# Accumulating DMAs at the end of the expert mixture, and normed rows stored in k-tile order

## The chip, the core and the metric

The kernel runs on one core of one Trainium2 chip. The metric is device time in microseconds (us) of one execution, median of several runs. Five engines work side by side, each through its own queue in order: TensorE (PE, with its weight loads as PEld), VectorE (DVE), ScalarE (ACT), GpSimd (POOL) and SyncE (SP), which here only issues DMAs. Sixteen DMA engines move data between DRAM and SBUF.

## What is computed

Two stacks one after the other on 512 tokens of width 1024, all in f32. The change touches the first stack, two layers of attention followed by a mixture of experts:

```python
for l in range(DEPTH):                       # DEPTH = 2
    ...                                      # three kinds of attention, concatenated to mix
    x = layer_norm(DEEPNORM_ALPHA * x + einsum('bsm,md->bsd', mix, w_out[l]), ln1_g[l], ln1_b[l])
    x = layer_norm(DEEPNORM_ALPHA * x + moe_ffn(x, w_router, router_bias, w_gate[l], w_up[l], w_down[l]), ln2_g[l], ln2_b[l])

def moe_ffn(x, ...):                         # 16 experts of width 256, two of them for each token
    scores = sigmoid(xt @ w_router)
    ...                                      # best group of four experts, best two in it, gates that sum to 1
    h = silu(einsum('nd,edf->enf', xt, w_gate)) * einsum('nd,edf->enf', xt, w_up)
    y = einsum('enf,efd->nd', h * gates, w_down)
```

The second stack (pooling, dilated attention, four wide feed-forward blocks) follows and is not touched.

## The kernel before, in words

Tokens lie in four tiles `t` of 128 rows (`X[:, t, :]`, 128x1024 f32). Most products are made of three passes (`mm3`, L205): weights are split by ACT and DVE into a high and a low part (`split`, L201 to L203; the tile is called `hl`), and TensorE does high by high, high by low, low by high. Plain f32 products and transposes go through TensorE directly.

A mixture layer (`moe`, L625) runs in four steps.

Route (L694 to L709): as soon as a tile of `X` is normed, SP stores it to DRAM (`x1d`, L699), TensorE transposes its eight 128x128 blocks (L705), ACT copies them to `x1T` (L706), and TensorE multiplies with the router's weights (L708). `x1T` lives in buffers tagged `xg`, four in the first layer and three in the second (`XG`). The choice of experts then runs on DVE with small products, up to `tok_of`, the list of rows for each expert.

Experts (L903 to L914): for each of 16 experts POOL gathers up to 96 rows of `x1d` with an indirect DMA (L823), `turn` (L827) transposes them in eight pieces, `widen` (L839) makes gate and up, `shift` (L871) transposes the 96x256 result in two pieces, `narrow` (L881) multiplies with `w_down`, ACT scales by the gates, and POOL scatters the rows to `yd` in DRAM (L893): the first choices in rows 0 to 511, the second choices in rows 512 to 1023. Weights are loaded so that a partition holds neighbouring rows (`"(p k) m"`, L680), so the piece `k` of a gathered row is every eighth of its elements, and the piece `f` of `h1` every second:

```python
xg = xgs.pop(e).rearrange("p (q k) -> p k q", k=KD)      # L829
PE.transpose(ps[...], xg[:, 4 * h + k, :], ident)        # L834
h1 = h1.rearrange("p (q f) -> p f q", f=2)               # L874
PE.transpose(ps[...], h1[:, f, :], ident)                # L876
```

Combine (L926 to L932): eight PSUM banks `acc[t, h]` are started with alpha times X (L924). For each tile `t` and each choice `j` SP loads 128 rows of `yd` (512 KB) and TensorE adds them to both halves `h` by a product with the identity (L932), 16 plain f32 products of 128x512 in a layer. The second choice's rows go to a buffer of `row_tile(t)` (L861): tags `y`, `y`, and for `t = 2` in the second layer `gain`, then `y` again. `self.hold` keeps the last of these loads; the weight loads of what follows (`wload`, L178) are issued behind it on SP's queue. All of `yd`'s loads wait for the last scatter.

Norm and feed (L934 to L942): `norm(t)` is bn_stats on both halves (L577), then a chain over DVE and POOL (L590, L591), or over DVE, ACT and POOL for tiles 1 and 2 of the first layer (L585 to L587). `feed(t)` (in the second layer after a second norm with `gain`) transposes the tile (L222) and splits it into `xt`, the operand of the next stage. The order is written out in `ENDS` (L42): first layer `c0 c1 n0 c2 n1 f0 c3 n2 f1 n3 f2 f3`, second `c0 c1 n0 n1 f0 f1 c2 c3 n2 n3 f2 f3`; a scheduler places the instructions of each engine within what the dependencies allow.

Of the kernel before, what the change touches and what calls it, by code (L numbers as in the profile page):

```python
# [9 lines left out]
F32 = mybir.dt.float32  # L10
# [4 lines left out]
OP = mybir.AluOpType  # L15
AX = mybir.AxisListType

P = 128
S = 512
T = S // P  # L20
D = 1024
KD = D // P
# [15 lines left out]
XG = 4, 3  # L38
# [12 lines left out]
CAP = 96  # L51
# [58 lines left out]
class Core:  # L110
# [514 lines left out]
    def moe(self, l, mix, mp, then):  # L625
        nc, a, c, tc = self.nc, self.a, self.c, self.tc
        V, A, PE, G = nc.vector, nc.scalar, nc.tensor, nc.gpsimd
# [47 lines left out]
        def fetch(n):  # L675

            for _ in range(n):
                w, e = need.pop(0)
                raw = next(places)
                src = a[w][l, e].rearrange("(p k) m -> p k m", p=P)  # L680
                k = src.shape[1] // 2
                if isinstance(raw, list):
                    ready[w, e] = [self.wload(src[:, h * k:(h + 1) * k], raw[h]) for h in range(2)]
                else:
                    v = self.wload(src, raw)
                    ready[w, e] = [v[:, :k], v[:, k:]]
# [7 lines left out]
        def route(t):  # L694

            X = self.X
            if t == 0:
                fetch(RAW + 5)
            nc.sync.dma_start(self.x1d[t * P:(t + 1) * P, :], X[:, t, :])  # L699
            lg = self.bank()[:NE, :P]  # L700
            x1T = mp.tile([P, KD, P], F32, name="x1T", tag="xg", bufs=XG[l])
            for h in range(2):
                ps = self.bank("t")
                for k in range(4):
                    PE.transpose(ps[:, k * P:(k + 1) * P], X[:, t, (4 * h + k) * P:(4 * h + k + 1) * P], self.ident)  # L705
                (V.tensor_copy if t == T - 1 and h else A.copy)(x1T[:, 4 * h:4 * h + 4, :], ps.rearrange("p (k q) -> p k q", q=P))  # L706
            for k in range(KD):
                PE.matmul(lg, wr[:, k, :], x1T[:, k, :], start=k == 0, stop=k == KD - 1)  # L708
            A.activation(scT[:, t * P:(t + 1) * P], lg, AF.Sigmoid)  # L709
        self.attn_out(l, mix, mp, route)  # L710
        X = self.X
# [40 lines left out]
        for t in range(T + 1):  # L752
            o = rk[:, t * NE:(t + 1) * NE]
# [14 lines left out]
        for j in range(2):  # L768
            for t in range(T):
                PE.matmul(sm_ps[:CAP, :3 * NE], hot[j][:, t, :], vals[:, j, t].rearrange("p a e -> p (a e)"),  # L770
                          start=j + t == 0, stop=j + t == T)
# [46 lines left out]
        xgs, ready_x = {}, {}  # L818
# [7 lines left out]

        def turn(e):  # L827

            xg = xgs.pop(e).rearrange("p (q k) -> p k q", k=KD)  # L829
            xgT = [mp.tile([P, KD, CAP], F32R, name=f"xgT{i}") for i in range(2)]  # L830
            for h in range(2):
                ps = self.bank("t")[:, :4 * CAP]
                for k in range(4):
                    PE.transpose(ps[:, k * CAP:(k + 1) * CAP], xg[:, 4 * h + k, :], self.ident[:CAP, :CAP])  # L834
                v = ps.rearrange("p (k q) -> p k q", q=CAP)
                self.split(xgT[0][:, 4 * h:4 * h + 4], xgT[1][:, 4 * h:4 * h + 4], v)
            ready_x[e] = xgT
# [23 lines left out]
        def row_tile(e):  # L861
            if e % 3 < 2:
                return mp.tile([P, D], F32, name="y", tag="y", bufs=2)
            if l == 0:
                return mp.tile([P, D], F32, name="y", tag="more2")
            return self.norm.tile([P, D], F32, name="y", tag="gain", bufs=2)
# [4 lines left out]
        def shift(e, h1):  # L871

            ps = self.bank("t")[:, :2 * CAP]
            h1 = h1.rearrange("p (q f) -> p f q", f=2)  # L874
            for f in range(2):
                PE.transpose(ps[:, f * CAP:(f + 1) * CAP], h1[:, f, :], self.ident[:CAP, :CAP])  # L876
            hT = [mp.tile([P, 2 * CAP], F32R, name=f"hT{i}", tag=f"hT{i}", bufs=2) for i in range(2)]
            self.split(hT[0], hT[1], ps)
            return e, hT
# [40 lines left out]
        acc = {}  # L920
        for t in range(T):
            for h in range(2):
                acc[t, h] = self.bank("at"[h])
                PE.matmul(acc[t, h], alpha, X[:, t, h * 512:(h + 1) * 512], start=True, stop=False)  # L924

        def combine(t):  # L926
            for j in range(2):
                yg = row_tile(t) if j else mp.tile([P, D], F32, name="yg", tag="xg", bufs=XG[l])
                i = nc.sync.dma_start(yg, self.yd[j * S + t * P:j * S + (t + 1) * P, :])
                self.hold = i.ins  # L930
                for h in range(2):
                    PE.matmul(acc[t, h], self.ident, yg[:, h * 512:(h + 1) * 512], start=False, stop=j == 1)  # L932

        def norm(t):  # L934
            with tc.issue_after(fed[1]) if t >= HOLD[l] else nullcontext():
# [40 lines left out]
    def rest_experts(self, l, mp, rp, slots):  # L976
        nc, a, tc = self.nc, self.a, self.tc
        V, A, PE, G = nc.vector, nc.scalar, nc.tensor, nc.gpsimd
        with tc.For_i(0, NE, 1) as e:
            one = bass.ds(e, 1)  # L980

            def weights(w, m, h):
                t = mp.tile([P, 1024], F32, name="wrest", tag="xg", bufs=XG[l])
                src = a[w][l, one].rearrange("o (k p) m -> p (o k) m", p=P)
                n = 1024 // m
                nc.sync.dma_start(t.rearrange("p (k m) -> p k m", m=m), src[:, h * n:(h + 1) * n, :])
                return t
# [502 lines left out]
```

## Time and profile before

| | |
|---|---|
| time, median of 3 runs | 2852.64 us (2850.58 to 2852.91) |
| the profiled execution | 2854.86 us, its span 2853.0 us |
| PE busy | 2761.9 us, 97% of the span |
| weight loads (PEld) busy | 2287.9 us, 80% |
| DVE, ACT, POOL busy | 1526.5, 1180.2, 233.0 us |
| chain that ended last | PE 63%, DVE 3%, ACT 1%, POOL 1% |
| TensorE's mean granted clock | 0.983 |

The profiled execution is 2.22 us above the median. Its span is the time from the first to the last instruction. A busy PE is not PE at its peak, since matmuls overlap; the pace of a row of equal instructions is read from the start of one to the start of the next.

### The profile page before, as it was taken

The numbers are of one execution on the slowest core, as the hardware profiler recorded it, in microseconds if no ns is written. First come the engines' busy times: TensorE is split into PE (matmuls) and PEld (weight loads), VectorE is DVE, ScalarE is ACT, GpSimd is POOL, SyncE is SP. The second block draws the span as 40 slices with busy tenths as digits, with TensorE's granted clock in tenths as the row PEclk, the third lists the DMA queues.
The fourth block names the chain that finished last, engine by engine and source line by source line (L and its number), as shares of the span: only waits on it lengthen the run. The fifth ranks groups of instructions, "written<-read, shape, count | busy, mean of one in ns | idle before, by whom it ended". The sixth has DMA issues, their size and how long they took to land.

```text
span 2853.0 us, 35973 instructions
## 1 busy us (share of the span) xinstructions
PE 2761.9 (97%) x14092; PEld 2287.9 (80%) x14092; DVE 1526.5 (54%) x2819; ACT 1180.2 (41%) x2133; POOL 233.0 (8%) x233
## 2 busy tenths in 40 slices
PE   8998999998999999999999999999999999999998
PEld 7767986766996888888888887998888787888886
DVE  7975987976896323356533337343233635632334
ACT  4373883373894222234423224232322445532222
POOL 0031211041211000010100001000000000100000
PEclk9999999999999999999999999999999999999999
DMA  4316976215985223323322333333232314133220
GB/s 168 76 45 228 349 274 216 60 39 218 322 334 194 99 90 104 101 68 125 98 94 89 104 103 108 133 122 104 90 102 94 106 42 138 52 104 103 95 93 33
DMA packets 176159, 365.06 MB, mean 128 GB/s; under 512 B 14544, under 2 KB 115152, under 8 KB 164592
## 3 DMA queue, kind: packets, MB, share of 16 engines
q1 hardware_dynamic: 165424, 336.35, 35.1%
q0 software_dynamic: 9984, 25.31, 2.6%
q8 instruction: 112, 1.84, 0.3%
q10 hardware_dynamic: 576, 1.05, 0.1%
q14 instruction: 63, 0.52, 0.1%
HBM read 343.73 MB, written 27.33 MB: 130 GB/s over the span
## 4 chain that ended last, share of the span: by engine, by line
PE 63%; DVE 3%; ACT 1%; issue 1%; POOL 1%; POOLq 0%; DVEq 0%; ACTq 0%
PE psa L207 17%; PE psa L209 17%; PE psa L208 17%; PE pst L207 3%; PE pst L209 3%; PE pst L208 3%; PE psa L1295 1%; PE pst L1323 1%; DVE xn L241 1%; POOL rr L1045 1%; DVE hl L203 1%; PE pst L222 1%; PE pst L1313 0%; DVE X L1060 0%; PE pst L1243 0%
## 5 line engine op out<-in xcount | busy, mean ns | idle before, releaser
L203 DVE TENSOR_TENSOR hl<-raw,hl 128x1024 fp32r<-128x1024 f32 (+2 forms) x451 | 552.6, 1232 | 776.5 <-ACT hl L202 774.3
L202 ACT CAST hl<-raw 128x1024 fp32r<-128x1024 f32 (+1 forms) x456 | 471.7, 1042 | 685.7 <-PE psa L209 331.6
L209 PE MATMUL psa<-xt,hl 128*128 128x512 f32 (+1 forms) x1632 | 603.9, 370 | 1.9 <-DVE hl L203 1.9
L207 PE MATMUL psa<-xt,hl 128*128 128x512 f32 (+1 forms) x1632 | 603.7, 370 | 0.7 <-ACT xt L202 0.7
L208 PE MATMUL psa<-xt,hl 128*128 128x512 f32 (+1 forms) x1632 | 604.1, 370 | 0.2 <-DVE xt L203 0.2
L209 PEld LDWEIGHTS psa<-xt,hl 128*128 128x128 f32 x1632 | 310.3, 190 | 53.8 <-DVE hl L203 2.3
L207 PEld LDWEIGHTS psa<-xt,hl 128*128 128x128 f32 x1632 | 310.1, 190 | 52.3 <-ACT xt L202 1.1
L208 PEld LDWEIGHTS psa<-xt,hl 128*128 128x128 f32 x1632 | 310.3, 190 | 51.8 <-DVE xt L203 0.8
L207 PE MATMUL psa<-hl,xt 128*128 128x512 f32 (+2 forms) x608 | 244.8, 404 | 3.1 <-ACT hl L202 3.1
L209 PE MATMUL psa<-hl,xt 128*128 128x512 f32 (+2 forms) x608 | 245.1, 403 | 0.0
L208 PE MATMUL psa<-hl,xt 128*128 128x512 f32 (+2 forms) x608 | 241.2, 397 | 3.1 <-DVE hl L203 3.0
L1096 ACT ACTIVATE silu<-psa 128x512 f32<-128x512 f32 x88 | 52.6, 597 | 345.8 <-PE psa L209 345.8
L207 PE MATMUL psa<-hl,hT 128*128 128x512 f32 (+1 forms) x480 | 189.0, 394 | 0.0
L208 PE MATMUL psa<-hl,hT 128*128 128x512 f32 (+1 forms) x480 | 187.8, 391 | 0.0
L209 PE MATMUL psa<-hl,hT 128*128 128x512 f32 (+1 forms) x480 | 187.8, 391 | 0.0
L1097 DVE TENSOR_TENSOR silu<-silu,psa 128x512 f32<-128x512 f32 x88 | 60.5, 687 | 218.3 <-PE psa L209 217.9
L1045 POOL TENSOR_TENSOR rr<-ms,consts 128x1 f32<-128x1 f32 x52 | 38.6, 744 | 1637.1 <-DVE ms L1043 1625.9
L207 PEld LDWEIGHTS psa<-hl,xt 128*128 128x128 f32 x608 | 139.2, 229 | 21.1 <-issue 3.3
L208 PEld LDWEIGHTS psa<-hl,xt 128*128 128x128 f32 x608 | 139.5, 229 | 18.6 <-DVE hl L203 5.3
L209 PEld LDWEIGHTS psa<-hl,xt 128*128 128x128 f32 x608 | 139.1, 229 | 13.3 <-issue 1.0
L207 PE MATMUL psa<-hl,xgT 128*96 128x256 f32 x512 | 145.5, 284 | 0.2
L209 PE MATMUL psa<-hl,xgT 128*96 128x256 f32 x512 | 143.3, 281 | 0.0
(365 smaller groups left out, 4420.6 us busy)
## 6 DMA issues: line engine op xcount, KB each, us to landing
raw<-in_ffn_w_gate_dram SPq DMA_DIRECT2D x44, 1024.0 KB
raw<-in_ffn_w_up_dram SPq DMA_DIRECT2D x44, 1024.0 KB
raw<-in_ffn_w_down_dram SPq DMA_DIRECT2D x44, 1024.0 KB
raw<-in_w_up_dram SPq DMA_DIRECT2D x16, 1024.0 KB
raw<-in_w_gate_dram SPq DMA_DIRECT2D x12, 1024.0 KB
raw<-in_w_down_dram SPq DMA_DIRECT2D x12, 1024.0 KB
xt<-in_w_down_dram SPq DMA_DIRECT2D x12, 1024.0 KB
xt<-in_w_gate_dram SPq DMA_DIRECT2D x10, 1024.0 KB
```

The source lines that it names most:

```text
L202: self.nc.scalar.copy(hi, src)
L203: return (self.nc.gpsimd if pool else self.nc.vector).tensor_tensor(lo, src, hi.bitcast(F32), op=OP.subtract)
L207: mm(out, lhs[0], rhs[0], start=start, stop=False)
L208: mm(out, lhs[0], rhs[1], start=False, stop=False)
L209: mm(out, lhs[1], rhs[0], start=False, stop=stop)
L222: self.nc.tensor.transpose(ps[:, k * P:(k + 1) * P], src[:, (4 * h + k) * P:(4 * h + k + 1) * P], self.ident)
L241: self.nc.vector.scalar_tensor_tensor(o, i, r, gh, op0=OP.mult, op1=OP.mult)
L1045: nc.gpsimd.tensor_tensor(r, ms, self.c("nhalf")[:, :1], op=OP.pow)
L1096: A.activation(s, acc[0], AF.Silu)
L1097: V.tensor_tensor(s, s, acc[1], op=OP.mult)
L1295: PE.matmul(ps[:, (j - j0) * nk + b * P:(j - j0) * nk + (b + 1) * P], qT[half(par), j, :], kv["k", g, kb][half(par), j, :], start=True, st ...
L1323: PE.matmul(o[half(par), j * P:(j + 1) * P], v[:, (2 * j + par) * 64:(2 * j + par + 1) * 64], pts[b][:, j * P:(j + 1) * P], start=b == 0, ...
```

## The change

- `route`: ACT copies each normed tile into a new tile `xp` (128x1024, tag `xg`) in which element `q * 8 + k` of a row stands at place `k * 128 + q`, and SP stores `xp` to `x1d` instead of `X`. The store now stands behind the copies to `x1T`.
- `turn` and `shift`: the transposes read pieces of 128 neighbouring elements. To fit, `w_down` is loaded as `"(k p) m"`: two runs of 4 KB for each partition in place of one of 8 KB.
- Combine: the four tiles of first choices are loaded into `sums[t]` (three buffers `xg`, one `y`), one load behind the other on SP; then POOL issues four DMAs that add the second choices' rows to them in SBUF (`accum_op=add`). TensorE adds one tile to each bank: 8 plain f32 products in a layer, not 16. `self.hold` is now the last of the four loads.
- `moe_rest` (only for experts with more than 96 rows) is adapted to the new order of rows.

```diff
-                src = a[w][l, e].rearrange("(p k) m -> p k m", p=P)
+                src = a[w][l, e].rearrange("(k p) m -> p k m" if w == "w_down" else "(p k) m -> p k m", p=P)
...
-            nc.sync.dma_start(self.x1d[t * P:(t + 1) * P, :], X[:, t, :])
...
+            xp = mp.tile([P, KD, P], F32, name="xp", tag="xg", bufs=XG[l])
+            A.copy(xp, X[:, t, :].rearrange("p (q k) -> p k q", k=KD))
+            nc.sync.dma_start(self.x1d[t * P:(t + 1) * P, :], xp.rearrange("p k q -> p (k q)"))
...
-            xg = xgs.pop(e).rearrange("p (q k) -> p k q", k=KD)
+            xg = xgs.pop(e)
...
-                    PE.transpose(ps[:, k * CAP:(k + 1) * CAP], xg[:, 4 * h + k, :], self.ident[:CAP, :CAP])
+                    PE.transpose(ps[:, k * CAP:(k + 1) * CAP], xg[:, (4 * h + k) * P:(4 * h + k + 1) * P], self.ident[:CAP, :CAP])
...
-            h1 = h1.rearrange("p (q f) -> p f q", f=2)
-                PE.transpose(ps[:, f * CAP:(f + 1) * CAP], h1[:, f, :], self.ident[:CAP, :CAP])
+                PE.transpose(ps[:, f * CAP:(f + 1) * CAP], h1[:, f * P:(f + 1) * P], self.ident[:CAP, :CAP])
...
+        sums = [mp.tile([P, D], F32, name="yg", tag="xg", bufs=XG[l]) if t < 3 else row_tile(0) for t in range(T)]
+        for t in range(T):
+            i = nc.sync.dma_start(sums[t], self.yd[t * P:(t + 1) * P, :])
+            self.hold = i.ins
+        for t in range(T):
+            G.dma_start(sums[t], self.yd[S + t * P:S + (t + 1) * P, :], accum_op=OP.add)
+
         def combine(t):
-            for j in range(2):
-                yg = row_tile(t) if j else mp.tile([P, D], F32, name="yg", tag="xg", bufs=XG[l])
-                i = nc.sync.dma_start(yg, self.yd[j * S + t * P:j * S + (t + 1) * P, :])
-                self.hold = i.ins
-                for h in range(2):
-                    PE.matmul(acc[t, h], self.ident, yg[:, h * 512:(h + 1) * 512], start=False, stop=j == 1)
+            yg = sums[t]
+            for h in range(2):
+                PE.matmul(acc[t, h], self.ident, yg[:, h * 512:(h + 1) * 512], start=False, stop=True)
```

## Rows read from the trace of the kernel before

**Rows 1.** Windows: stretch; us, busy time (instructions) of each engine, PEclk, DMA share, GB/s.

```profile
276.00:430.00 154.00, 153.64 (x1130) 139.24 (x1131) 131.60 (x164) 131.81 (x187) 27.74 (x29) 0.98 0.84 304
430.00:456.00 26.00, 23.42 (x61) 10.50 (x60) 11.56 (x21) 5.07 (x8) 5.38 (x6) 0.93 0.83 300
```

**Rows 2.** Groups by line and shape, PEld: count, busy us, mean ns, idle before.

```profile
L834 PEld LDWEIGHTS pst<-consts,xg 96*128 96x128 f32 x256 | 31.9, 203 | 13.0 <-issue 13.0
...
L876 PEld LDWEIGHTS pst<-consts,h 96*128 96x128 f32 x64 | 10.3, 196 | 0.2
...
L705 PEld LDWEIGHTS pst<-consts,X 128*128 128x128 f32 x64 | 7.2, 140 | 1.4 <-issue 0.8
```

**Rows 3.** Timeline of TensorE, bursts of transposes: start us, us, instruction, idle before.

```profile
254.26 1.58 PE L705 MATMUL pst<-consts,X 128*128 128x128 f32 x13
...
263.29 0.26 PEld L714 LDWEIGHTS psa<-consts,scoresT 16*128 16x128 f32 x3 [0.21 <-issue]
...
420.26 0.32 PEld L876 LDWEIGHTS pst<-consts,h 96*128 96x128 f32 x2
420.47 0.19 PEld L207 LDWEIGHTS psa<-hl,xgT 128*96 128x96 f32 x1
...
851.51 0.98 PEld L834 LDWEIGHTS pst<-consts,xg 96*128 96x128 f32 x8
852.38 0.19 PEld L207 LDWEIGHTS psa<-hl,hT 128*96 128x96 f32 x1
```

**Rows 4.** Timelines of ACT and POOL, route stage of the first layer.

```profile
252.46 1.05 ACT L202 CAST hl<-early 128x1024 fp32r<-128x1024 f32 x1 [3.18 <-PE pst L209]
...
258.37 0.58 ACT L706 COPY x1T<-pst 128x512 f32<-128x512 f32 x1 [0.21 <-PE pst L705]
...
260.80 0.58 ACT L706 COPY x1T<-pst 128x512 f32<-128x512 f32 x1 [0.32 <-PE pst L705]
...
271.92 1.25 POOL L823 DMA_INDIRECT xg<-x1d,tok_of  x1 [14.55 <-DVE tok_of L781]
```

**Rows 5.** Timelines of SP, PE and DVE, end of the first layer's mixture.

```profile
434.70 0.33 SPq L929 DMA_DIRECT2D yg<-yd  x1
...
444.16 3.31 SPq L188 DMA_DIRECT2D raw<-in_w_in_dram  x4
...
438.32 1.73 PE L932 MATMUL psa<-yg,consts 128*128 128x512 f32 x2 [2.05 <-DMA yg<-yd]
...
449.56 1.02 PE L932 MATMUL pst<-y,consts 128*128 128x512 f32 x2
450.42 0.60 PE L222 MATMUL pst<-consts,X 128*128 128x128 f32 x4
...
442.89 0.70 DVE L577 BATCH_NORM_STATS2 st<-psa 128x6 f32<-128x512 f32 x1 [15.31 <-PE psa L932]
...
446.29 1.28 DVE L591 SCALAR_TENSOR_TENSOR X<-X,rstd,gb 128x1024 f32<-128x1024 f32 x1
```

**Rows 6.** Timelines of PE, SP and DVE, end of the second layer's mixture.

```profile
875.90 1.12 PE L932 MATMUL psa<-yg,consts 128*128 128x512 f32 x2 [2.00 <-DMA yg<-yd]
...
886.50 0.33 SPq L247 DMA_DIRECT2D gain<-in_norm_gain_dram  x1
...
878.78 0.70 DVE L577 BATCH_NORM_STATS2 st<-psa 128x6 f32<-128x512 f32 x1 [13.57 <-PE psa L932]
...
893.66 0.68 DVE L249 TENSOR_SCALAR gain<-gain 128x1024 f32<-128x1024 f32 x1
894.26 1.22 DVE L203 TENSOR_TENSOR hl<-raw,hl 128x1024 fp32r<-128x1024 f32 x1
```

**Rows 7.** Windows (columns as in the first group), after the first combine load landed.

```profile
438.00:440.00 2.00, 1.68 (x3) 0.78 (x4) 0.00 (x0) 0.00 (x0) 0.00 (x0) 0.68 1.03 420
```

**Rows 8.** Tile `x2d`: POOL's 512 KB stores, ns min/median/max, then time to landing.

```profile
L942 POOL DMA_DIRECT2D x2d<-X x4: 538/594/630, 447.9 to 465.9; - x4
...
DMA to landing us min/median/max: 3.5/5.4/7.3
```

More of the change, by code (lines that the diff above doesn't have):

```diff
@@ L983, in weights @@
                 t = mp.tile([P, 1024], F32, name="wrest", tag="xg", bufs=XG[l])
-                src = a[w][l, one].rearrange("o (k p) m -> p (o k) m", p=P)
+                src = a[w][l, one].rearrange("o (k p) m -> p (o k) m" if w == "w_down" else "o (p k) m -> p (o k) m", p=P)
                 n = 1024 // m
```

## The prediction

> **What bounds the kernel now.** The page says TensorE, 97% busy, and the chain that ended last is mostly PE. That is an average, so the second view is the one by stage. In the experts' stretch PE is busy 153.64 of 154 us, ACT 131.81, DVE 131.60, and the DMA engines have a share of 0.84 [rows 1]; the second layer's stretch, 714 to 868 us, repeats it. There every instruction that leaves TensorE shortens the kernel, until ACT or DVE, 14% below, become the bound. In the 26 us at the end of the first mixture PE is busy 23.42 us and DVE 11.56 [rows 1], but the timeline shows an order in it: PE waits 2.05 us for the first rows of `yd`, DVE waits 15.31 us for the first finished bank, and only then does the chain of norms start which the next stage needs [rows 5]. The second layer has the same start: the first rows at 875.90, the first norm at 878.78 [rows 6]. So two questions decide: how much TensorE's work with the experts shrinks, and how much later the first norm starts when the rows go through two DMAs in a row.
>
> **Part by part: the transposes with the experts.** In `turn` eight pieces are transposed, in `shift` two. Their weight loads take 203 and 196 ns, while the loads of the same kind from neighbouring elements in `route` take 140 ns [rows 2]. The starts show what that costs: eight loads of L834 from 851.51 until the next line's load at 852.38, 0.109 us each, and two of L876 from 420.26 to 420.47, 0.105 us each [rows 3]. What would they take with neighbouring elements? The loads alone can follow each other much faster: three of L714, also 128 columns, in 0.26 us with some 0.14 for the last, about 0.06 us apart [rows 2, 3]. Then the moving side is the bound. `route`'s 13 transposes move 128 columns and take 1.58 us [rows 3], four of the same shape 0.60 [rows 5], so nine more cost 0.98 us, 0.109 each; with 96 columns that is 0.109 x 96 / 128 = 0.082 us. The gain is 8 x 0.027 + 2 x 0.023 = 0.26 us for an expert, and 8.4 us for 16 experts in two layers. ACT (131.81 us) and DVE (131.60) stay below PE's new 150 us a layer, and the weights would be wanted at 304 x 154 / 150 = 312 GB/s, where 420 were seen [rows 1, 7]. Bounds: nothing, if the pace is not set by these loads; 32 x 10 x (0.108 - 0.06) = 15 us, if it were set by loads alone. I take 8.4, since L705 is the same instruction on 128 columns.
>
> The strided loads are also where a rule of the Trainium skill differs from a row. L834 steps 32 bytes and L876 8 bytes, and both are slow (203 and 196 ns) [rows 2]. By the Trainium skill, SBUF — State Buffer, section "Door 1: The DMA port swizzle" (the note on cachelines), a step within a line of 16 bytes, up to four f32, is free. By that rule L876 would gain nothing and the sum would be 1.5 us worse; the trace disagrees, so I count it.
>
> **The route stage.** Four ACT copies of 128x1024 a layer are added; ACT's cast of that shape takes 1.05 us [rows 4]. Seven of the eight lie in ACT's idle time between the copies to `x1T`. The last tile's can collide: ACT ends the copy for the tile before at 258.95, waits for PE and starts the last tile's at 260.80 [rows 4], and X is ready about 259, so 1.05 us just fits. In the second layer there are three buffers, and `xp` may have to wait for one; then up to 0.7 us is late. If a strided read halves ACT's rate as it does the weight loads, the copy takes 2.1 us and each layer loses 1 to 1.7 us. I take 0.3 a layer, 0.6 us in all, with 0 to 3.4. Nothing below 0, since only work is added here. The store to `x1d` now waits for ACT, and one weight load stands behind the last store on SP's queue, 1 to 2 us later; no row shows PE waiting for a weight there. The gathers start at 271.92 after the list of rows [rows 4]; a store issued at 261 with the longest landing of a 512 KB store, 7.3 us [rows 8], is there by 268.5. That cover is 3.4 us; were it gone, the first gather would be late one for one.
>
> **`w_down` in runs of 4 KB** instead of 8: the rows of `yd` are runs of 4 KB and move at 420 GB/s [rows 7], above what the stage wants. Zero.
>
> **The combine.** Removed: 8 of 16 plain products a layer at 0.86 us (449.56 to 450.42) [rows 5], 6.9 us of PE a layer. None of it lies before the first norm except one tile's two. Added: a second DMA between the load and the first product. Call `x` the time from POOL's issue of the first accumulating DMA to its landing. The trace has no such DMA. Nearest are POOL's plain stores of the same 512 KB: 3.5, 5.4, 7.3 us (min, median, max) [rows 8]. They bound `x` from below at 3.5. It will not find the DMA engines free: from 438 us on they have a share of 1.03 at 420 GB/s [rows 7], and SP's queue now holds the other three loads, and behind them the next stage's weights, because `hold` passes after four loads, at about 436.5, instead of 444.16 [rows 5]. From above I take twice the median, 10.8 us, if each added row costs a read of both operands. I take 6.2, between median and maximum of the plain stores. POOL has nothing else queued then: the first `rstd` needs a bank that itself needs `x`, so the four waiting DMAs block nobody.
>
> First layer: rows land at 438.32 as before, the sum at 438.4 + x. PE then has been idle about 8 us; after 2 us of idleness the granted clock was 0.68 of full in 438 to 440 [rows 7], so part of it ran at the lower of the two levels, 1.2 GHz, and the first pair of instructions took 1.73 us [rows 5]. So the first bank is ready at 438.4 + x + 1.7, against 442.89 [rows 5]: x - 2.8 later. Against that: X of tile 0 was ready at 446.29 + 1.28 = 447.57 but its transposes came at 450.42, behind the products of tile 2 [rows 5]. Half of those are gone, and the next weights are there 7 us earlier, so PE can start the next stage between the feeds. I take 2 us of these 2.85. Net x - 4.8, that is +1.4 us.
>
> Second layer: 875.95 + x + 1.7 against 878.78 [rows 6], x - 1.1 later. Here DVE is the chain from 878.78 on, and removing PE's work behind it gives nothing. What it gains: the load of `gain` waited until 886.50 for a buffer that the second choices' rows held [rows 6]; now it is free. Its scaling (0.68 us) and the first split behind it (until 895.48) stand in the chain from 893.66 [rows 6], 1.8 us that can move ahead. Net x - 2.9, that is +3.3 us.
>
> The later sums follow in 2.5 us each if half of 420 GB/s goes to POOL's queue; a norm takes DVE 4.7 us (442.89 to 447.57) [rows 5], so only the first one counts.
>
> **Sum.** -8.4 + 0.6 + (2x - 7.7) = 2x - 15.5. With x = 6.2 it is -3.1 us. Against the profiled execution 2854.86 - 3.1 = 2851.8; against the median, 2.22 us lower, 2849.5 us.
>
> **The rivals.** A measurement of this kernel can tell about 0.2%, 5.7 us, from no change.
>
> Fast additions (faster): x is 3.5 to 4.9, like a store that meets little traffic. 2 x 3.5 - 15.5 = -8.5, so 2844 us. For it: the queues are separate, and POOL's shortest store took 3.5. Against it: the share of 1.03. If the loads alone set the transposes' pace, up to 6.6 us more go.
>
> Additions that pay for two reads (slower): x is 10.8 and more, and the sums follow each other at 5 us, longer than a norm. 2 x 10.8 - 15.5 = +6.1, with up to 3 us more for the last tile: 2859 to 2862 us. It decides from x = 10.6 on. For it: the traffic; against it: the longest plain store took 7.3.
>
> That is also a rule: in the Trainium skill, Collectives: The Full Stack, section "The bandwidth ceiling: the fold count and why AG ≠ RS ≠ AR", an adding DMA emits two reads for one write and delivers half as much. No row here shows an adding DMA.
>
> The strided loads are not what sets the pace (the change doesn't do what it says): then 8.4 us are missing, 2849.5 + 8.4 = 2858 us. For it only that L834's 0.109 is by chance also `route`'s pace for 128 columns; against it, that L834 moves only 96.
>
> **How the numbers follow.** Forecast, a small gain within 0.2% (x from 4.9 to 10.6): 0.44; its own range 2847 to 2856. Faster by over 0.2%: 0.36, nearly all by fast additions. Slower: 0.20, 0.13 for two reads and 0.07 for the transposes. Predicted 2849.5 us. The range takes in x = 3.5 (2844) with some of the transposes' upper bound, and x = 10.8 (2859): 2842 to 2860.
>
> **What would show it.** Right: L834's loads near 140 ns and the experts' stretch 4 us shorter in each layer; POOL's accumulating DMAs landing about 6 us after issue; the first bn_stats of each end 2 to 5 us later after the last scatter; `gain` loaded before the first norm. Wrong: an experts' stretch of unchanged length, a first norm that starts no later, or PE waiting at the third or fourth tile's sum. The sum itself fails most easily in x, which enters twice.

## The result, and the profile after

The changed kernel takes 2879.4 us (median of 4 runs, 2877.34 to 2883.46) against 2852.8 in the same series: a ratio of 1.0098, 95% interval 1.0086 to 1.011. Forecast were 2849.5 us, range 2842 to 2860. The profiled execution took 2883.46 us (span 2881.3), 28.6 us more than that of before.

Where did it go? Five marks of the timelines divide the first stack: the first transposes of gathered rows, the last scatter of each mixture (POOL's last issue to `yd`), SP's reload of `X` in the next layer, and the first `silu` of the second stack. A stretch is the difference between two marks, in us:

| | start to first transposes | experts 1 | end 1 (last scatter to reload of X) | reload to first transposes | experts 2 | end 2 (last scatter to first silu) | first silu at |
|---|---|---|---|---|---|---|---|
| before | 276.24 | 155.02 | 149.57 | 133.64 | 154.42 | 47.38 | 916.27 |
| after | 278.44 | 151.97 | 167.83 | 135.26 | 151.29 | 62.69 | 947.48 |
| difference | +2.2 | -3.1 | +18.3 | +1.6 | -3.1 | +15.3 | +31.2 |

So the experts gain 6.2 us, the two route stages lose 3.8, and the two ends lose 33.6. Behind the first silu the program is the same; that part took 1936.7 us before, 1933.8 after, and 1931.7 to 1940.6 in the profiled executions below, with no relation to the change. That is why the experiments are compared by stretches as well as by times. Each stretch comes from one execution, which lies within 6 us of its kernel's median (13 us over it in the second run of experiment 8), so the difference of a single stretch below 3 us is not read by itself. The five kernels with the old combine and no late load (before, the first of experiment 1, the last of experiment 8, both of experiment 9) give the scatter of the ends: 197.0 to 201.2 us for both together, so a sum over both ends is read only beyond some 4 us.

By windows (columns as in [rows 1]) the same stretches of after:

```profile
276.00:430.00 154.00, 151.32 (x1132) 136.45 (x1133) 132.96 (x167) 132.73 (x188) 29.71 (x30) 0.97 0.85 306
430.00:456.00 26.00, 13.69 (x25) 5.08 (x23) 3.42 (x7) 1.93 (x3) 4.54 (x6) 0.74 0.86 231
```

In the second one TensorE is busy for 13.69 us instead of 23.42, DVE for 3.42 instead of 11.56, at a granted clock of 0.74, with fewer GB/s at a higher DMA share.

The transposes first. Groups by line and shape of after, weight loads (count, busy us, mean ns), to be held against [rows 2]; L837 and L878 are the old L834 and L876:

```profile
L837 PEld LDWEIGHTS pst<-consts,xg 96*128 96x128 f32 x256 | 25.2, 145 | 13.2 <-issue 13.2
...
L878 PEld LDWEIGHTS pst<-consts,h 96*128 96x128 f32 x64 | 8.3, 141 | 0.3
```

203 and 196 ns have become 145 and 141. The starts, against [rows 3] (timeline of the weight loads of after):

```profile
846.55 0.26 PEld L878 LDWEIGHTS pst<-consts,h 96*128 96x128 f32 x2
846.76 0.16 PEld L207 LDWEIGHTS psa<-hl,xgT 128*96 128x96 f32 x1
...
849.47 0.75 PEld L837 LDWEIGHTS pst<-consts,xg 96*128 96x128 f32 x8
850.17 0.16 PEld L207 LDWEIGHTS psa<-hl,hT 128*96 128x96 f32 x1
```

In `turn` a load now follows the other after 0.087 us instead of 0.109 (0.082 forecast). The pair of `shift` keeps its 0.105 from load to load, but its two matmuls and the gap behind them take 0.111 us instead of 0.146 (medians of the 32 pairs, from the first one's start to that of the next product). ACT in the route stage of after, against [rows 4]:

```profile
255.25 1.06 ACT L705 COPY x1T<-pst 128x512 f32<-128x512 f32 x2
256.21 2.09 ACT L708 COPY xp<-X 128x1024 f32<-128x1024 f32 x1
258.18 0.61 ACT L705 COPY x1T<-pst 128x512 f32<-128x512 f32 x1
258.66 2.09 ACT L708 COPY xp<-X 128x1024 f32<-128x1024 f32 x1
```

A permuting copy takes 2.09 us, twice ACT's 1.05 for that shape, and the copies to `x1T` wait behind it.

Now the end of the first mixture, to be held against [rows 5]. Timeline of POOL: the four accumulating DMAs.

```profile
437.71 0.99 POOL L934 DMA_DIRECT2D yg<-yd  x1 [6.39 <-DMA yg<-yd]
439.08 0.89 POOL L934 DMA_DIRECT2D yg<-yd  x1 [0.38 <-issue]
441.39 0.86 POOL L934 DMA_DIRECT2D yg<-yd  x1 [1.42 <-DMA yg<-yd]
442.66 0.85 POOL L934 DMA_DIRECT2D y<-yd  x1 [0.42 <-issue]
```

Timeline of TensorE:

```profile
447.11 2.07 PE L939 MATMUL psa<-yg,consts 128*128 128x512 f32 x2 [11.69 <-DMA yg<-yd]
...
456.71 1.12 PE L939 MATMUL psa<-y,consts 128*128 128x512 f32 x2 [1.25 <-DMA y<-yd]
457.67 1.02 PE L939 MATMUL pst<-y,consts 128*128 128x512 f32 x2
458.97 0.65 PE L222 MATMUL pst<-consts,X 128*128 128x128 f32 x4 [0.28 <-DVE X L591]
459.47 0.60 PE L222 MATMUL psa<-consts,X 128*128 128x128 f32 x4
468.66 1.11 PE L222 MATMUL pst<-consts,X 128*128 128x128 f32 x4 [8.60 <-POOL X L587]
...
470.28 0.73 PE L207 MATMUL psa<-hl,xt 128*128 128x452 f32 x1
```

From POOL's issue (437.71) to the first product (447.11) x is 9.4 us; in the second layer 9.15 (893.67 to 902.82). TensorE then waits a second time, 8.60 us, for tile 1, and the first product of the next stage comes 39.9 us after the last scatter (430.41), before 25.0 (456.28 after 431.26). What holds up the norms stands in the timelines of DVE

```profile
453.98 1.10 DVE L203 TENSOR_TENSOR hl<-raw,hl 128x904 fp32r<-128x904 f32 x1 [2.35 <-ACT hl L202]
454.99 0.20 DVE L579 BATCH_NORM_AGGREGATE mv<-st 128x2 f32<-128x12 f32 x1
```

and of ACT:

```profile
453.00 1.79 ACT L202 CAST hl<-raw 128x904 fp32r<-128x904 f32 x2 [22.86 <-DMA raw<-in_w_in_dram]
457.78 1.80 ACT L202 CAST hl<-raw 128x904 fp32r<-128x904 f32 x2 [2.99 <-DVE st L577]
```

The statistics of tile 0 are aggregated only when a split of the next stage's weights, which had to land first, is done: the scheduler had put it ahead, since the weights pass earlier now. The second layer, against [rows 6]: TensorE waits 13.02 us for the first sum,

```profile
902.82 2.08 PE L939 MATMUL psa<-yg,consts 128*128 128x512 f32 x2 [13.02 <-DMA yg<-yd]
```

and ACT's squares for the first feed (L1048) stand behind such casts:

```profile
911.75 1.04 ACT L202 CAST hl<-raw 128x1024 fp32r<-128x1024 f32 x1 [27.23 <-DMA raw<-in_ffn_w_gate_dram]
914.74 1.99 ACT L202 CAST hl<-raw 128x1024 fp32r<-128x1024 f32 x2 [1.95 <-DMA raw<-in_ffn_w_up_dram]
916.64 0.62 ACT L1048 ACTIVATE junk<-X 128x512 bf16<-128x512 f32 x1
```

And the DMA engines, by windows (columns as in [rows 1]), while only additions and weights move, against the 420 GB/s of [rows 7]:

```profile
443.00:447.00 4.00, 0.00 (x0) 0.00 (x0) 0.00 (x0) 0.00 (x0) 0.52 (x1) 0.50 1.05 241
```

They are full (1.05) at 241 GB/s, and TensorE's granted clock has gone to the lower of its two levels, 0.50 or 1.2 GHz.

### The profile page after: what moved, and what is told of

Same layout as the page of the kernel before. It is cut to its first block, busy times and chain, and to the rows that moved or that the text cites. A ratio compares the mean times of both kernels' runs of the same rounds, so it can differ in the third digit from the quotient of the medians.

```text
span 2881.3 us, 35932 instructions
## 1 busy us (share of the span) xinstructions
PE 2748.3 (95%) x14060; PEld 2277.3 (79%) x14060; DVE 1525.5 (53%) x2819; ACT 1195.8 (42%) x2141; POOL 241.4 (8%) x241
## 3 DMA queue, kind: packets, MB, share of 16 engines
q10 hardware_dynamic: 576, 1.05, 0.1%
```

## Experiments

Results are times (median, ratio to the kernel before with 95% interval) and the stretches named above.

**1. The two parts by themselves.** The k-tile order with the old combine; then the new combine with the old transposes.

> The k-tile order alone: rows permuted on ACT ahead of the store, w_down in two runs, pieces of neighbouring elements in turn and shift; the combine is that of the kernel before. Theory: this part still brings what the trace of the changed kernel shows in it: its experts' stretch is 3.05 us shorter in the first layer, after a route stage that is 2.2 us longer, because the permuting copy takes 2.04 to 2.14 us where an ACT pass over 128x1024 from neighbouring elements took 1.05. With about -4 us of experts a layer and +2.2 of route that is -3 to -4 us: 2849 to 2850 us. Rival: the route stage and the two runs of w_down take back all of it, 2852 to 2856 us.

2851.0 us, 0.9997 (0.9987 to 1.0007). Experts 150.50 and 151.14 us (-4.5, -3.3); first transposes at 278.45 (+2.2) and 135.62 us behind the reload (+2.0). The stretches bear the theory out: a gain, half of it paid back in the route stage. The gain stands in the other kernels too: the experts of the second layer take 150.5 to 151.5 us in the twelve other profiled kernels that have the k-tile order, and 154.1 to 155.4 in the three that have the old one. The time doesn't show it: 2851.0 lies between the two ranges, and the interval, -3.7 to +2.0 us, only just takes in the -3 to -4 of the theory. End 2 was 3 us longer with the same combine; some 1.7 us of that is a lower clock behind the wait for the first rows (experiment 8).

> The accumulating DMAs alone: combine as in the changed kernel, transposes, w_down and the store to x1d as in the kernel before. Theory: the whole loss sits at the two ends of the mixture, so this kernel is slower than the changed one by what the k-tile order brings there: 2852.8 + 26.6 + 3.5 = 2883 us (2880 to 2886). Rival: the loss comes only when both parts meet (an earlier end of the experts, another order in the queues): 2860 to 2870 us.

2887.7 us, 1.0127 (1.0105 to 1.015): a little more than the theory. Experts as before (155.03, 155.41), end 1 164.15, end 2 62.26. The loss sits in the ends, and the combine alone makes it.

**2. Adding or only loading.** The same DMAs without the addition.

```diff
-            G.dma_start(sums[t], self.yd[S + t * P:...], accum_op=OP.add)
+            G.dma_start(sums[t], self.yd[S + t * P:...])
```

> The changed kernel with the second choices' DMAs as plain ones: same queue (POOL's), same tiles, same dependence on the first load, but they overwrite instead of adding, so the sum of the two choices is left out. Theory 1, adding itself is what is slow: POOL's issue to landing falls from 9.4 to 12.6 us to 4 to 7 us, the weights behind come sooner, and the time falls by 2 x 4 us or more: 2862 to 2872 us. Rival, the place is what is slow (a second load in a row, against the weights on SP's queue): issue to landing stays over 8.5 us and the time at 2877 to 2881 us.

2872.5 us, 1.0078 (1.0054 to 1.0102). The first load lands 6.7 us after its issue (7.1 in the second layer), so the addition costs 2 to 2.7 us of x, and later ones more; ends 163.11 and 57.00. That is theory 1, half a microsecond above its range. But 13.5 and 9.6 us of loss remain without any adding. So with the queues as they are in the changed kernel the adding is worth 10.4 us of the ends (230.5 to 220.1) and 6.9 us of the time; experiment 7 asks the same with another order.

**3. The order of the queues, first try.** Weight splits behind the feed of tile 1 at both ends (`x` stands for its last instructions on ACT, DVE and POOL).

```diff
+        with tc.issue_after(x):
             self.split(hi, lo, src, pool)
```

> The changed kernel with the first four splits of the next stage's weights queued behind the feed of tile 1 on ACT, DVE and POOL, at both ends of the mixture; nothing else is changed. Theory, order of the queues: of the loss at each end only some 3 us more than forecast come from the late sum, and 6 to 8 us come from norms and feeds that stand behind splits of weights that have not landed: the time falls by 10 to 16 us, 2863 to 2870 us. Rival, the chain of two DMAs and the low clock behind its idle time are all: the splits are off the path, the time stays within 3 us of the changed kernel, 2876 to 2882 us, or rises, because the splits are now late for TensorE.

2879.7 us, 1.0097 (1.0075 to 1.0119): the theory as I put it fell; the time is the rival's, and so is the reason, as the first layer shows. In the second layer the first feed came 30.5 us after the last scatter instead of 36.9 and end 2 shrank to 59.72. In the first layer the splits were now late for TensorE: its first product came at 43.5 us, not 39.9, and end 1 stayed (166.53). TensorE itself also had an order that cost: it stood at the fourth tile's sum while tile 0 was ready.

**4. Weights held back, alone.** SP sends 16 numbers of the first sum to DRAM, and the weight loads stand behind that.

```diff
+        self.hold = nc.sync.dma_start(self.mark[l:l + 1, :], sums[0][0:1, 0:16]).ins
```

> The changed kernel with the next stage's weights held back at both ends: SP first sends 16 numbers of the first finished sum to DRAM, and the weight loads stand behind that. Theory, contention: the weights that SP sends behind the four loads slow the additions; without them the first addition lands 5 to 7 us after its issue instead of 9.1 to 9.4, the last one is in 3 us or more sooner, and the time falls by 6 to 12 us: 2867 to 2873 us. Rival, an adding DMA takes that long by itself, among its own kind: the first lands after 8.5 us or more, and the weights that now come later cost what is gained: 2878 to 2888 us.

2879.3 us, 1.0092 (1.0063 to 1.0121); ends 169.13 and 63.90. The first addition landed in 7.8 and 8.0 us instead of 9.4 and 9.15, and nothing came of it. That is the rival's time, but neither's x. Its windows show additions among themselves, with no weights moving:

```profile
437.00:439.00 2.00, 0.00 (x0) 0.00 (x0) 0.00 (x0) 0.00 (x0) 0.87 (x2) 0.50 1.05 195
439.00:441.00 2.00, 0.00 (x0) 0.00 (x0) 0.00 (x0) 0.00 (x0) 0.83 (x1) 0.50 1.04 188
```

The DMA engines are full at 190 GB/s, less than half of the 420 of plain loads in [rows 7]: this is what the rival of two reads said of the rate.

**5. No chain.** Second choices by plain DMAs beside the first choices', TensorE adds both; then the same with the orders of experiment 6.

> The changed kernel with the second choices' rows loaded by plain DMAs on POOL's queue into tiles of their own, beside the first choices' on SP's, and both added by TensorE (16 products a layer as before). The weights still pass behind the fourth load on SP. Theory, the two DMAs in a row are the cause: without the chain the first product starts 7 to 9 us after the last scatter (before 7.1, changed 16.7), and the time is that of the k-tile order alone within 6 us: 2849 to 2857 us. Rival, the early weights and the order of queues that follows from them are a cause of their own: the first product is early but the feeds are late, 2862 to 2872 us.

> The kernel with plain loads of the second choices on POOL's queue and both tiles added by TensorE, with the same orders put back by hand as in the run above. Theory, order and chain are all there is: without the chain and with the order mended, the first layer's end (last scatter to the reload of X in the next layer) is within 4 us of the 149.6 us of before, and the time is 2851 to 2859 us. Rival, the weight loads that pass early on SP's queue cost by themselves, because the second choices' rows share the DMA engines with them: over 2863 us.

2872.6 us, 1.0071 (1.0054 to 1.0088), and 2867.3, 1.0053 (1.0037 to 1.0069). Both theories of the chain failed: the first product came after 7.2 us, but ends were 163.87 and 54.50, and 159.89 and 55.69. The times are those of the rivals (0.6 us over its range in the first). But the runs do not price the early weights: in the second kernel the third and fourth second-choice load wait for a buffer until 13.4 and 15.9 us after the scatter, and then share the DMA engines with the weights, so TensorE waits again (timeline of TensorE, the second kernel):

```profile
451.66 2.07 PE L949 MATMUL psa<-y,consts 128*128 128x512 f32 x2 [5.32 <-DMA y<-yd]
```

Issued at 442.36, that load took 9 us; before, all eight loads of rows stand ahead of the weights. A kernel without the chain, with the orders put back and the weights behind all eight loads, was not run.

**6. The order of the queues, whole.** In the first layer TensorE adds tile 3 behind the feed of tile 0, splits stand behind the norm of tile 1; in the second behind the feed of tile 1.

```diff
+            with tc.issue_after(fed["pe"]) if l == 0 and t == T - 1 else nullcontext():
                 for h in range(2):
                     PE.matmul(acc[t, h], self.ident, yg[...], start=False, stop=True)
```

> The changed kernel with the orders of the kernel before put back by hand: in the first layer TensorE adds the fourth tile only behind the feed of tile 0, and the next stage's weight splits stand behind the norm of tile 1; in the second they stand behind the feed of tile 1. The accumulating DMAs stay. Theory: the order of the queues is the larger part of the loss. The feed of tile 1 in the first layer comes 31 to 33 us after the last scatter instead of 38.2, the first product of the next stage 32 to 35 us instead of 39.9; the time falls by 10 to 15 us: 2864 to 2870 us. Rival, the order only shifts the waiting, since the weights land late as well: first product at 38 us or later, time 2875 to 2881 us.

2873.7 us, 1.0080 (1.0064 to 1.0096). TensorE in the first layer, last scatter at 427.81:

```profile
453.56 0.66 PE L228 MATMUL pst<-consts,X 128*128 128x128 f32 x4 [0.71 <-DVE X L598]
...
462.11 1.11 PE L228 MATMUL pst<-consts,X 128*128 128x128 f32 x4 [5.74 <-POOL X L594]
463.02 1.06 PE L228 MATMUL psa<-consts,X 128*128 128x128 f32 x4
463.73 0.73 PE L213 MATMUL psa<-hl,xt 128*128 128x452 f32 x1
```

Tile 1 is fed 34.3 us after the scatter (38.2 in after, 31 to 33 expected), the first product comes after 35.9 (39.9). Ends 160.19 and 59.93: 7.6 and 2.8 us of the 33.6 were the order, by these executions. The time fell by 5.7, less than the 10 to 15 of the theory, to between its range and the rival's, and the intervals of the two ratios (1.0086 to 1.011 and 1.0064 to 1.0096) still touch.

**7. What is left, with that order.** Weights held as in 4; and plain loads as in 2.

> The changed kernel with the orders put back by hand, and also the weights held behind the first sum by the small DMA on SP. Theory: with the order right, the weights that pass early are the next cause: the first sum lands in 8 us instead of 9, the later ones 2 to 3 us sooner, and both ends together (last scatter to the reload of X, and to the first silu) shrink by 4 us or more against 160.2 and 59.9 us: about 2868 to 2870 us. Rival: weights that come later cost as much as the sums gain: ends together within 3 us of 220.1 us, 2872 to 2876 us.

> The changed kernel with the orders put back by hand and plain DMAs in place of the adding ones (the sum of the two choices is left out). It prices the adding itself where no order is in the way. Theory: a sum that lands 2.3 us sooner, and later ones 5 us sooner, shorten each end by 2.5 to 5 us: ends together 210 to 215 us against 220.1, 2863 to 2869 us. Rival: adding is not what the ends wait for: within 3 us of 220.1 us.

Held weights: 2872.8 us, 1.0075 (1.0051 to 1.0098); ends 157.46 and 56.92, together 214.4 against 220.1, so 5.7 us, little more than the scatter of the ends. The ends follow the theory; the time is the rival's, with 5 us more behind the first silu than in experiment 6. Its first addition lands in 5.6 us (tile `yg`, first layer):

```profile
L942 POOL DMA_DIRECT2D yg<-yd x3: 854/890/984, 437.9 to 440.4; - x3
...
DMA to landing us min/median/max: 5.6/8.4/10.0
```

Plain loads: 2873.3 us, 1.0086 (1.0065 to 1.0106); ends 159.22 and 59.20, together 218.4. That is 1.7 us, within what can't be read, and the rival's: where the order is right, no price of the adding itself can be measured here.

The three kernels with the chain and with the orders put back show what the ends follow. How much later than before the first product stands behind the last scatter (before: 7.06 and 7.01 us), and how much longer the ends are, in us:

| | first product later, end 1, end 2 | end longer, end 1, end 2 |
|---|---|---|
| experiment 6 | 9.7, 10.6 | 10.6, 12.6 |
| plain loads | 8.4, 8.7 | 9.7, 11.8 |
| held weights | 6.5, 8.2 | 7.9, 9.5 |

Each end is longer by what the first product is late, and 0.9 to 3.2 us more. The rows of the held weights, TensorE:

```profile
443.56 2.07 PE L949 MATMUL psa<-yg,consts 128*128 128x512 f32 x2 [8.50 <-DMA yg<-yd]
...
889.12 2.08 PE L949 MATMUL psa<-yg,consts 128*128 128x512 f32 x2 [10.23 <-DMA yg<-yd]
```

**8. A late first sum, and the clock.** The kernel before, its first rows loaded twice; then products of zeros that keep TensorE busy in its wait, ten in the changed kernel and two in the k-tile order with later permuting copies.

```diff
+        for n in range(10):
+            PE.matmul(acc[n % 4, n % 2], zeros, X[...], start=False, stop=False)
```

> The kernel before, with one change: the first rows of each combine are loaded twice into the same tile, the second time only when the first has landed, so that all that follows at both ends is some 4 us later; no adding, no POOL queue, no other order. It tests the step in which the forecast let 2 us of a late first sum vanish at each end. Theory, one for one: each end is longer by what the first product is later (about 4 us), 2858 to 2862 us. Rival, the relief of the forecast: each end takes up 2 us of it, 2854 to 2857 us.

2869.4 us, 1.0069 (1.0053 to 1.0086): more than either said. The first product is 3.3 and 3.75 us later, the ends 4.5 and 9.6 us longer (154.06, 57.00). TensorE in the first layer shows the first half of that:

```profile
442.42 3.78 PE L933 MATMUL psa<-yg,consts 128*128 128x512 f32 x4 [5.36 <-DMA yg<-yd]
445.99 1.40 PE L933 MATMUL pst<-yg,consts 128*128 128x512 f32 x2
447.23 1.02 PE L933 MATMUL psa<-y,consts 128*128 128x512 f32 x2
```

A product is two instructions here. Behind the wait two products take 3.6 us, 1.8 each, where later ones follow in 0.86: the lower level, half of the upper. In the second layer the first statistics are then 7.5 us late (17.38 against 9.89), and the second feed waits 5.18 us more for DVE, which split weights first. So "no other order" holds in the first layer only. In the second TensorE does all products ahead of the first feed, which comes 27.5 us after the scatter (901.36); before it stood among the products of tile 3, 18.4 us after it (887.32). The 9.6 us are thus lateness, clock and order together; the 4.5 for 3.3 in the first layer are the clean reading.

> The changed kernel with ten products of zeros by X added to the open banks behind those with alpha, at both ends, so that TensorE works during most of the wait for the first sum; the result is unchanged. Theory, the clock takes part of the loss: the first products then stand 0.86 us apart instead of 1.7 to 1.9, the first norm starts 2 us sooner at each end, and the time falls by 4 to 6 us: 2873 to 2876 us. Rival, the norms wait for the later sums and for queues anyway: less than 2 us, 2877 to 2881 us.

2883.5 us, 1.0104 (1.0081 to 1.0127): no gain, and over both ranges. Ten products left 3.12 us of the wait. The granted clock was still full in the 4 us with the wait and fell to 0.57 in the next 4; the first products stood 1.9 us apart again:

```profile
445.00:449.00 4.00, 1.45 (x4) 0.38 (x2) 0.00 (x0) 0.00 (x0) 1.02 (x2) 1.00 1.04 249
449.00:453.00 4.00, 3.43 (x5) 1.38 (x6) 0.70 (x1) 0.00 (x0) 0.00 (x0) 0.57 1.06 243
```

> The k-tile order with the late permuting copies, combine as before, and two products of zeros by X behind those with alpha, which fill most of the 2 us in which TensorE waits for the first rows at each end; the result is unchanged. Theory, those 2 us are what lets the clock fall: the first products stand 0.86 us apart at both ends (before: 1.7 at one end, 0.86 at the other), the first bank statistics come 9.9 to 10.2 us after the last scatter at both ends instead of 11.6, and the time is 2 to 3 us below that of the kernel without them, 2847 to 2850 us. Rival, the level there does not hang on this wait: one or both ends at 11.5 us or more, 2850 to 2854 us.

2853.7 us, 1.0014 (1.0005 to 1.0024). The theory of the clock fits, its time does not. With 0.42 and 0.17 us of wait left the products stand some 0.86 us apart at both ends, and the first statistics come 10.04 and 9.78 us after the last scatter; before, the same wait of 2 us was followed by the lower level in one layer and not in the other [rows 5, 6]. But these are two ends of one execution: of the eight ends with that wait (before, the first of experiment 1, both of experiment 9) five had the first statistics after 11.4 to 11.7 us and three after 9.9 to 10.0. The time is the rival's. In this execution the first transposes came at 280.51, of which the late copies explain a part (experiment 9), and end 1 took 153.52, for which I found no reason.

**9. Versions without the loss.** The k-tile order with the permuting copies later on ACT; and natural order with gate and up loaded in runs of 1 KB, without a copy.

> The k-tile order alone, as in the first run, with each permuting copy moved on ACT behind the next tile's copies to x1T, and the last two behind the last sigmoid; combine as before. Theory, the copies cost only because they stand ahead of the last tile's x1T copies: the first transposes of gathered rows are at 276.0 to 276.8 us again instead of 278.45, the experts keep their 7.8 us, and the time is 2845 to 2849 us. Rival, the last store to x1d now comes too late for the first gather: the first transposes at 278 us or later, 2850 to 2853 us.

> Neighbouring elements for the transposes without the permuting copy: X is stored as it is, as in the kernel before, gate and up are loaded in the order that fits it, in runs of 1 KB instead of 8, w_down in runs of 4 KB; combine as before. Theory: the experts keep their 7.8 us (the sum of both layers with the k-tile order alone) and the route stage loses nothing: 2844 to 2848 us against 2852.3. Rival: with runs of 1 KB the weights come too slowly for TensorE and the experts' stretch gets longer than the 155.0 us of before: over 2856 us.

2852.4 us, 1.0000 (0.9987 to 1.0012), and 2849.6, 0.9995 (0.9984 to 1.0005). With later copies the first transposes came at 276.49 in the first layer, but in the second not sooner (135.58 behind the reload). The 276.49 is no gain of the route: the attention ahead of it was 2.8 us shorter in that execution. A nearer mark shows it, the last bank statistics of the norm ahead of the route. Late copies, first layer (timelines of DVE and TensorE):

```profile
252.43 0.69 DVE L577 BATCH_NORM_STATS2 st<-X 128x6 f32<-128x512 f32 x1
...
276.49 1.51 PE L845 MATMUL pst<-consts,xg 96*128 96x96 f32 x8 [7.82 <-DMA xg<-x1d,tok_of]
```

Behind that mark the first transposes come after 24.1 and 23.9 us here, after 21.0 to 21.5 in the four kernels without permuting copies (before, the second of experiment 1, the first of experiment 8, the second of experiment 9), and after 22.4 to 23.3 in the eleven with the copies where the change put them. So the copies cost about 2.0 and 1.5 us where the change put them, and more when moved: the list of rows comes 1.5 us later, the first gather starts 0.6 us later behind it and lands 0.5 to 0.8 us later. The theory fell, and the time is the rival's. The rival's cause, the last store too late for the gather, can be in the last two terms, which are half of the 2.6 to 3.0 us over before. With runs of 1 KB the route stages lose nothing (275.37, 132.72), but the experts take 152.97 and 156.33 us. The DMA engines are then full at 322 to 344 GB/s in the middle of both stretches, where the k-tile order moved 358 to 379, and TensorE idles for 3 of the 25 us from 810 on: the weights are late instead, as the rival had it, though the time, between the two ranges, stayed under its 2856 us. No version is measurably faster than the kernel before.

## Why the prediction was wrong

**The transposes** were right in mechanism and size: -8.4 us forecast, -7.8 in experiment 1, -6.2 in the profiled execution of after. `shift`'s loads, which step 8 bytes, fell from 196 to 141 ns. By the Trainium skill, SBUF — State Buffer, section "Door 1: The DMA port swizzle", they should have had nothing to gain; the trace disagrees, as I had counted, though the gain is smaller than counted: 0.035 us a pair (0.146 to 0.111), 1.1 us in all instead of 1.5.

**The route stage** was mis-sized: 0.6 us taken, 4.2 measured in experiment 1, some 3.5 by the nearer mark of experiment 9. The prediction named the case (a strided read halves ACT's rate, 2.1 us a copy) and priced it at 1 to 1.7 us a layer; it happened at 1.5 to 2.2. In after the copies stand ahead of later tiles' `x1T` copies too, not only of the last one's. The stores' cover held in after: the first gather starts 1.0 us behind the list of rows, as before.

**x** was 9.4 and 9.15 us, not 6.2, inside its bounds of 3.5 and 10.8. By the sum that is 2 x 9.3 - 15.5 = +3.1 us, and with the route's 3.6 more 6.7: of the 26.6 us by the medians, this is the smaller part. One term was missing beside x: the first addition was issued 7.3 and 8.9 us after the last scatter, where the rows had been at TensorE after 7.1 and 7.0, so 1.9 us of the second layer's delay come before x begins. The rival of two reads, chance 0.13, was right on the rate: 190 GB/s at full DMA engines in experiment 4. The Trainium skill, Collectives: The Full Stack, section "The bandwidth ceiling: the fold count and why AG ≠ RS ≠ AR", states two reads and half as much delivered for the reducing step of a collective; the rate here agrees with that. It was not what decided: adding cost 10.4 us of the ends with the queues of the changed kernel (experiment 2) and nothing that can be read with the order put back (experiment 7), and at x = 10.8 the sum would still have been only +6.1.

**The step that failed is the one that turns x into time**: "net x - 4.8" and "net x - 2.9". With the orders put back and the weights held, x was 5.7 and 6.6, my own value, and by these terms the ends should have cost 0.9 + 3.7 = 4.6 us. They cost 7.9 + 9.5 = 17.4, or some 13 against the longest ends that the old combine showed. Three errors are in it.

First, the relief. I counted removed products as time won, and took 2 us because TensorE could start the next stage between the feeds. But TensorE was 23.42 us busy of 26 there before [rows 1]: it had work because the rows came early and one after the other. When the first sum comes 6 to 11 us later it has none, and the wait is lost one for one and a little more (the table of experiment 7; in experiment 8 3.3 us late cost 4.5 in the first layer). Of the 13.8 us of products that were removed nothing shows in the ends.

Second, the clock. I charged the lower level to one pair of instructions. The first products of after stand 1.7 to 1.9 us apart instead of 0.86, as in [rows 5], and the level falls a second time behind the wait for tile 1, where the next stage's first product takes 0.73 us instead of 0.45 (456.28 in the timeline of before). This is the smallest of the three: the first statistics stand 2.1 us behind the first product in both layers, where 1.7 were taken.

Third, and not in the prediction at all, the order of the queues. I wrote that weights which are there 7 us earlier help, and that POOL's waiting DMAs block nobody. POOL's did not. But the earlier `hold` let the scheduler put the weight splits ahead of norms on ACT and DVE, and tile 3's sum ahead of tile 0's feed on TensorE, in queues that run in order, while on the chip the weights came late, since they shared the DMA engines with the additions. That is 10.4 us by experiment 6, and holding the weights is another 5.7 by experiment 7, which is just what the first products come sooner by (3.3 and 2.4 us).

So of the 33.6 us lost at the ends, 10.4 are the order, 5.7 the weights beside the additions, and 17.4 are left with both mended. Of these 17.4, 14.7 are what the first products are still late (6.5 and 8.2 us), the second transfer in a row; the other 2.7 are not divided. The clock behind the wait can be in them, and the norm of tile 1 still stood behind statistics of tile 2 on DVE and the store to `x2d` on POOL, which was not tried apart. This division goes by single executions. The medians agree on the direction and give back less: 2879.4, then 2873.7 with the orders put back, then 2872.8 with the weights held too, still 21 us over the kernel before.

**What would show it** was half useful: the first statistics came 7.2 and 10.3 us later after the last scatter (18.81 against 11.63, 20.14 against 9.89), over the 2 to 5 named; `gain` was loaded ahead of the first norm, as said, and nothing that it won can be seen. One of the signs of being wrong came too: TensorE waited 1.25 us for the fourth tile's sum in the first layer, and 0.44 and 1.00 us for the third and fourth in the second.

## What to carry to other kernels

Where everything behind a load waits for it, a second transfer in a row costs its whole latency, as it did here; products that it saves count only where TensorE has other work at that moment. When a change lets loads pass earlier, look at what else the scheduler will then queue ahead of the norms, and ask whether those loads will have landed by the time the chip comes to it. Before an operation moves from an engine to a DMA, look at the share of the DMA engines in that stretch.

## What was not expected of the hardware

An accumulating DMA of 512 KB took 5.6 us at the least (experiment 7) and 8.8 to 12.3 beside weight loads (experiments 1 and 6, tile `yg`, first layer); the DMA engines were full at 190 GB/s with it, 420 without. A copy on ACT that reads every eighth f32 took 2.02 to 2.14 us for 128x1024, 1.05 from neighbouring elements. POOL's issue of an accumulating DMA took 0.85 to 1.01 us, 0.53 to 0.63 for a plain one. A wait of 2 us before the first products was followed by the lower clock level at five of eight ends and not at the other three, with 1.4 to 1.8 us between them.
